# A decoder block on one core: state-space output with two matrices per group, a split gated product, constants loaded by SyncE, and new instruction orders

## The chip, the cores and the metric

The kernel runs on one core of one Trainium2 chip. The metric is the device time of one execution in microseconds (us). Before the change three runs gave 1078.19, 1079.68 and 1080.48, a median of 1079.68 us. A further execution was taken with the hardware profiler; all profile lines of the kernel before come from that one.

The names of the engines in the profile: PE is TensorE (matmuls), PEld its weight loads, DVE is VectorE, ACT is ScalarE, POOL is GpSimd, SP is SyncE, which here only issues DMAs.

## The reference

One layer of a decoder, float32, 512 tokens of width 1024:

```
h = h + 1/2 * SwiGLU_1(RMSNorm(h))                 # 1024 -> 2816 -> 1024
z = RMSNorm(h) @ W_in                              # q | k/v cmp, slc, win | gates | u (512 channels)
o = concat(NSA(8 heads x 64), S5(32 groups x 16 channels)) @ W_out
h = h + o
h = h + 1/2 * SwiGLU_2(RMSNorm(h))
h = h + sigmoid(RMSNorm(h) @ W_gate) * (p @ W_ple)
out = RMSNorm(h)
```

The S5 part, which the change is about, is for each of 32 groups a diagonal complex recurrence with 64 states, then a gelu and a gated linear unit:

```
state_t = a_bar * state_(t-1) + (B u_t) * b_coef   # complex, per group
y_t = Re(state_t) @ C_re^T - Im(state_t) @ C_im^T + d_skip * u_t
y = gelu(y);  out = y * sigmoid(y @ w_glu + b_glu) # w_glu is 512 x 512
```

## The kernel before, in words

**Layout.** Activations lie transposed: a tile of 128 features on the partitions by 512 tokens. The residual stream `h` is 8 such tiles. Weights come in `unit`s of 128 x 1024 fp32 (eight blocks of 128 x 128) from a packed tensor, loaded by SP into a ring of four buffers (`load_unit`, L111).

**Precision.** A product is done in a reduced fp32 type in three parts: `split` (L151, L152) makes `hi` by a cast on ACT and `lo` as the rest on DVE; the other operand is split the same way; `mm3` then does hi x hi, hi x lo, lo x hi. A product of two unsplit fp32 operands is the other way: the profile shows such a product as two records.

**Stages.** First FFN (to about 355 us), input projection with rotary products, key and value projections and the S5 input (to about 460), S5 interleaved with the score products (462 to 514), the gated linear unit (523 to 539), attention values and the output projection (from 544), second FFN (to 1011), the gate and the final norm. In the FFN most hidden tiles use a seven-product scheme, `prepare`, in which POOL issues DMAs that load weights and add a weight tile onto another (`raw<-raw`, L360).

**S5.** Time is cut in 64 chunks of 8 steps. The constants are computed on the chip in the first FFN, written to DRAM, and loaded again chunk by chunk: `s5i` holds per group a 128 x 128 input matrix `fd`, and cosines and sines `cd`, `sd` of 64 columns; `s5o` holds three 128 x 128 matrices `md`, `gd`, `gs` per group, where `gs` is `gd` with its two 64-partition halves exchanged (written by extra DMAs). `s5_in(j)` takes four groups at a time, eight times over: two loads by POOL (`si` of 512 KB, `so` of 768 KB, L886 and L888), a product with u (PE, `ps_C<-u,si`), a rotation by cos and sin on DVE (L894 to L897), the recurrence by four scans (L900) into `vv`, and one operation that multiplies `vv` by cos and by sin into the two halves of `z` (L904). `s5_out` adds per group three fp32 products, u with md, z cos with gd, z sin with gs. So the exchange of real and imaginary halves is done by the matrix `gs`. `vv` and the rotation's tiles have one buffer each, `si` three, `z` two.

**Gated unit.** `glu` takes four gelu tiles `yt` of 128 x 512, two raw weight units and 16 plain fp32 products of 512 columns (`ps_A<-yt,raw`); then tanh on ACT, and the gated tiles are split into `oh`, `ol` (L1092, L1094) for the output projection.

**What sets the order.** The program is traced first, and then `impose` chains each engine's instructions in the order that a table of numbers, `ENGINE_ORDER`, gives (L1627); a second table, `TILE_ORDER`, orders some users of shared buffers. So every engine, the two DMA issuers SP and POOL too, runs through a fixed list, and an instruction that waits holds back all that stand behind it on its engine. `rsqrt_steps` (L315 to L322) is the chain of a norm: `ones,acc` sums squares on PE, `ms` on DVE, `ri` on POOL, `nt`, `ri`, `dg` on DVE, and `dg,ones` on PE spreads the result.

Of the kernel before, what the change touches and what calls it, by code (L numbers as in the profile page):

```python
# [76 lines left out]
def block_kernel(ctx: ExitStack, tc: tile.TileContext, a: dict, out: bass.AP):  # L77
# [420 lines left out]
    s5i = dram.tile([128, NG, 256], F32, tag="s5i", name="s5i")  # L498
    fd, cd, sd = (s5i[:, :, i:j] for i, j in ((0, 128), (128, 192), (192, 256)))
    s5o = dram.tile([128, NG, 384], F32, tag="s5o", name="s5o")  # L500
    md, gd, gs = (s5o[:, :, i:j] for i, j in ((0, 128), (128, 256), (256, 384)))
    r8 = pers.tile([128, NG], F32, name="r8")

    def s5_constants(sp):
        if True:
# [175 lines left out]
            def make_m(c):  # L681
# [3 lines left out]
                for r in (0, 64):  # L685
                    nc.sync.dma_start(gs[64 - r:128 - r, chunk(c)], ko[r:r + 64])
# [30 lines left out]
            for c in range(2):  # L717
                gs_ = slice(16 * c, 16 * c + 16)
                tcs = sp.tile([128, 2, 16, 64], F32, tag="big0", name="tcs")
# [23 lines left out]
                nc.sync.dma_start(cd[:, gs_], tcs[:, 0])  # L743
                V.tensor_scalar(tcs[:, 1], tcs[:, 1], pos, None, OP.mult)
                nc.sync.dma_start(sd[:, gs_], tcs[:, 1])
# [48 lines left out]
    def mixer(ctx):  # L794
# [76 lines left out]
        for i in range(2):  # L871
            raw = tp.tile([128, SEQ], F32, tag=f"r{i + 1}", name="rope")
            nc.gpsimd.dma_start(raw, a["rope"][:, i])
            ropes.append(raw)
# [5 lines left out]
        zs = [s5w.tile([128, 2, GC, 64], F32, name="z", bufs=1, tag=f"z{i}") for i in range(2)]  # L880
        for z in zs:
            G.memset(z[:, :, :, 0:1], 0.0)

        def s5_in(j):
            si_ = s5w.tile([128, GC, 256], F32, tag="si", name="si", bufs=3)
            G.dma_start(si_, s5i[:, GC * j:GC * j + GC])  # L886
            so = s5w.tile([128, GC, 384], F32, tag="so", name="so")
            G.dma_start(so, s5o[:, GC * j:GC * j + GC])  # L888
            co, si = si_[:, :, 128:192], si_[:, :, 192:256]
            w = bank(TW, (128, GC, 64))  # L890
            for g in range(GC):
                mm(w[:, g], si_[:, g, 0:128], u8[:, GC * j + g], True, True)
# [10 lines left out]
            cs_ = si_.rearrange("p g (a c) -> p a g c", c=64)[:, 2:4, :, 0:63]  # L903
            V.tensor_tensor(z[:, :, :, 1:64], vv[:, None, :, 0:63].to_broadcast([128, 2, GC, 63]), cs_, OP.mult)  # L904
            return so, z

        def s5_out(j, yc, so, z):

            y = bank(TY, (128, GC // 2, 128))
            for i in range(GC // 2):  # L910
                for n, lhs in enumerate((u8[:, GC * j:GC * j + GC], z[:, 0], z[:, 1])):
                    for p in range(2):
                        g = 2 * i + p
                        mm(y[64 * p:64 * p + 64, i], lhs[:, g], so[:, g, 128 * n:128 * n + 128], n == 0, n == 2)
# [162 lines left out]
        def glu():  # L1077
            for m in range(4):
                yt = yts[m]
                gelu2(yt, yt, SEQ, ("r1", "r2")[m % 2])  # L1080
            yield
            for m in range(4):
                if m % 2 == 0:
                    raw = unit(True)
                o = bank("A")
                for k in range(4):
                    q = (m * 4 + k) % 8
                    mm(o, raw[:, q * 128:(q + 1) * 128], yts[k], k == 0, k == 3)
# [301 lines left out]
    with tc.tile_pool(name="gate", bufs=2, reuse_waits="tile") as gp:  # L1390
# [400 lines left out]
```

## Time and profile before

| what | value |
|---|---|
| median of three runs | 1079.68 us (1078.19 to 1080.48) |
| the profiled execution's own time | 1081.65 us |
| its span | 1079.9 us |
| busy: PE, DVE, ACT, POOL | 1042.9 (97%), 808.2 (75%), 521.9 (48%), 94.8 (9%) |
| granted TensorE clock, mean | 0.986 |
| moved by DMA | 151.13 MB, mean 140 GB/s |

A busy time is the sum over an engine's instructions; an average over the span mixes stages with different limits, which is why the prediction reads windows. In a timeline row stand start, duration, engine, line, operation, the names of what is written and read, shape, count, and in brackets the idle time before it with what ended it. In a row of groups stand busy us and mean ns, then the idle time before the group's instructions. PEclk is the clock that the chip granted to TensorE, as a share of full speed.

### The profile page before, as it was taken

What the parts mean: (1) busy time and instruction counts of PE and PEld (TensorE: products, weight loads), DVE (VectorE), ACT (ScalarE), POOL (GpSimd) and SP (SyncE); (2) the same over time, 40 slices, a digit from 0 to 9 for tenths busy, and PEclk for the clock granted to TensorE, in tenths of its full rate; (3) what the DMA queues carried; (4) which work ended last, traced back from release to release, by engine and by line L of the source; (5) the groups of instructions that cost most, each with busy time, mean ns of one, the idle gap of its engine ahead of it and who ended that gap; (6) DMA issues with size and microseconds to landing.
All of it is one profiled execution on the core that took longest, in us unless ns stands there. A gap on an engine that the chain in (4) does not pass through costs nothing.

```text
span 1079.9 us, 16852 instructions
## 1 busy us (share of the span) xinstructions
PE 1042.9 (97%) x6446; PEld 902.7 (84%) x6446; DVE 808.2 (75%) x1339; ACT 521.9 (48%) x911; POOL 94.8 (9%) x118
## 2 busy tenths in 40 slices
PE   6999999999999999999999999999999999999895
PEld 4788899799898888777577677998999899898795
DVE  7999876977887685699678968775576476476675
ACT  5334265335435532356789736463355245255431
POOL 5000010010001110011000001101011010100000
PEclk9999999999999999999899999999999999999898
DMA  9333356975747647867200066356356356445202
GB/s 313 108 94 110 82 152 158 252 183 136 205 109 187 222 133 206 210 212 251 66 32 20 15 210 175 93 142 179 84 143 178 91 117 160 114 122 172 59 30 69
DMA packets 86624, 151.13 MB, mean 140 GB/s; under 512 B 27648, under 2 KB 47104, under 8 KB 86544
## 3 DMA queue, kind: packets, MB, share of 16 engines
q1 hardware_dynamic: 72544, 120.23, 36.0%
q0 software_dynamic: 13152, 29.66, 13.5%
q8 instruction: 50, 0.82, 0.3%
q10 hardware_dynamic: 848, 0.17, 0.1%
q14 instruction: 30, 0.25, 0.1%
HBM read 123.27 MB, written 17.83 MB: 131 GB/s over the span
## 4 chain that ended last, share of the span: by engine, by line
PE 46%; issue 3%; DVE 2%; ACT 2%; POOLq 0%; POOL 0%; DVEq 0%; DMA 0%; SPq 0%; ACTq 0%
PE ps_C L130 13%; PE ps_A L130 13%; PE ps_B L130 12%; PE ps_D L130 8%; ACT hi L151 1%; DVE lo L152 0%; ACT pu L375 0%; DVE ple L1430 0%; DVE h L1107 0%; DVE h L478 0%; DVE acc L184 0%; ACT sq L183 0%; ACT eh L1242 0%; ACT e L1238 0%; DVE dg L322 0%
## 5 line engine op out<-in xcount | busy, mean ns | idle before, releaser
L151 ACT CAST hi<-raw 128x1024 fp32r<-128x1024 f32 (+2 forms) x201 | 208.7, 1042 | 260.2 <-PE ps_C L130 116.6
L152 DVE TENSOR_TENSOR lo<-raw,hi 128x1024 fp32r<-128x1024 f32 (+2 forms) x201 | 245.4, 1228 | 78.7 <-ACT hi L151 76.2
L130 PE MATMUL ps_C<-hq,hi 128*128 128x512 f32 x704 | 219.4, 393 | 0.7 <-DVE hq L345 0.2
L130 PEld LDWEIGHTS ps_C<-hq,hi 128*128 128x128 f32 x704 | 130.0, 189 | 28.2 <-DVE h L478 1.6
L130 PE MATMUL ps_A<-xh,hi 128*128 128x256 f32 (+1 forms) x456 | 143.1, 314 | 7.7 <-ACT xh L173 7.7
L130 PE MATMUL ps_A<-xl,hi 128*128 128x256 f32 (+1 forms) x456 | 142.2, 312 | 2.7 <-DVE xl L174 2.7
L130 PE MATMUL ps_A<-xh,lo 128*128 128x256 f32 (+1 forms) x456 | 142.3, 312 | 0.9 <-DVE lo L152 0.9
L130 PE MATMUL ps_C<-hq,lo 128*128 128x512 f32 x352 | 137.5, 391 | 0.0
L130 PEld LDWEIGHTS ps_A<-xh,hi 128*128 128x128 f32 x456 | 87.4, 192 | 12.9 <-ACT xh L173 7.7
L130 PEld LDWEIGHTS ps_A<-xl,hi 128*128 128x128 f32 x456 | 87.4, 192 | 9.3 <-DVE xl L174 4.0
L130 PEld LDWEIGHTS ps_A<-xh,lo 128*128 128x128 f32 x456 | 87.4, 192 | 6.0 <-DVE lo L152 1.4
L130 PE MATMUL ps_B<-sh,hi 128*128 128x256 f32 x280 | 81.1, 290 | 2.4 <-ACT pu L375 1.0
L130 PE MATMUL ps_B<-sh,lo 128*128 128x256 f32 x280 | 78.7, 281 | 0.2 <-DVE lo L152 0.2
L130 PE MATMUL ps_B<-sl,hi 128*128 128x256 f32 x280 | 78.6, 281 | 0.0
L130 PEld LDWEIGHTS ps_C<-hq,lo 128*128 128x128 f32 x352 | 66.4, 189 | 14.0
L478 DVE SCALAR_TENSOR_TENSOR h<-ps_C,h 128x512 f32<-128x512 f32 x64 | 44.2, 691 | 41.6 <-PE ps_C L130 40.3
L354 POOL DMA_DIRECT2D raw<-in_wpack x35 | 31.9, 910 | 408.1 <-DVE acc L184 131.6
L130 PE MATMUL ps_D<-sh,hi 128*128 128x256 f32 x220 | 62.1, 282 | 0.2 <-ACT p L375 0.2
L130 PE MATMUL ps_D<-sh,lo 128*128 128x256 f32 x220 | 62.1, 282 | 0.0
L130 PE MATMUL ps_D<-sl,hi 128*128 128x256 f32 x220 | 61.8, 281 | 0.0
L130 PEld LDWEIGHTS ps_B<-sh,hi 128*128 128x128 f32 x280 | 52.7, 188 | 6.7 <-ACT pu L375 5.4
L130 PE MATMUL ps_B<-xh,hi 128*128 128x512 f32 (+1 forms) x164 | 58.0, 353 | 0.1
(402 smaller groups left out, 2320.9 us busy)
## 6 DMA issues: line engine op xcount, KB each, us to landing
raw<-in_wpack SPq DMA_DIRECT2D x172, 512.0 KB, 4.3
raw<-in_wpack POOLq DMA_DIRECT2D x35, 256.0 KB, 4.7
raw<-raw POOLq DMA_DIRECT2D x35, 256.0 KB, 3.3
so<-s5o POOLq DMA_DIRECT2D x8, 768.0 KB, 6.7
si<-s5i POOLq DMA_DIRECT2D x8, 512.0 KB, 7.7
h<-in_xT SPq DMA_DIRECT2D x8, 256.0 KB, 5.5
s5i<-fs SPq DMA_DIRECT2D x4, 512.0 KB, 5.8
s5o<-gt SPq DMA_DIRECT2D x4, 512.0 KB, 4.7
```

Of the source, the lines that this page charges most:

```text
L130: return PE.matmul(o, lhsT, rhs, start=start, stop=stop, **kw)
L151: S.copy(hi[:, c], raw[:, c])
L152: V.tensor_tensor(lo[:, c], raw[:, c], hi[:, c].bitcast(F32), OP.subtract)
L354: nc.gpsimd.dma_start(a0[:, 1], src[:, 0:512], accum_op=OP.add)
L478: V.scalar_tensor_tensor(h[:, m, :], o, 0.5, h[:, m, :], OP.mult, OP.add)
```

## The change

1. **S5 output.** `z` becomes one rotated state: z = vv cos + x, where x is vv sin with its two 64-partition halves exchanged. DVE does it in four operations (L904 to L907) with a new tile `zt` in one buffer. `s5o` has two matrices, `gs` and its DMAs are gone, and `s5_out` does two products per group.
2. **Constants.** `s5i` becomes two tensors, the input matrices `s5f` and the cosines and sines `s5t`; the latter is written by two DMAs of 1 MB instead of four of 512 KB. The loads in `s5_in` (`fi`, `ti`, `so`, three buffers each, 256, 256 and 512 KB) and the two rotary tables are issued by SP instead of POOL.
3. **Gated unit.** The two weight units and the four gelu tiles are split into hi and lo, and the 16 products go by `mm3`: 48 matmuls.
4. **Orders.** Both tables are new for all five engines.

```diff
@@ constants
-    s5i = dram.tile([128, NG, 256], F32, tag="s5i", name="s5i")
-    fd, cd, sd = (s5i[:, :, i:j] for i, j in ((0, 128), (128, 192), (192, 256)))
-    s5o = dram.tile([128, NG, 384], F32, tag="s5o", name="s5o")
-    md, gd, gs = (s5o[:, :, i:j] for i, j in ((0, 128), (128, 256), (256, 384)))
+    fd = dram.tile([128, NG, 128], F32, tag="s5f", name="s5f")
+    td = dram.tile([128, NG, 2, 64], F32, tag="s5t", name="s5t")
+    s5o = dram.tile([128, NG, 256], F32, tag="s5o", name="s5o")
+    md, gd = (s5o[:, :, i:j] for i, j in ((0, 128), (128, 256)))
...
-                for r in (0, 64):
-                    nc.sync.dma_start(gs[64 - r:128 - r, chunk(c)], ko[r:r + 64])
...
-                nc.sync.dma_start(cd[:, gs_], tcs[:, 0])
                 V.tensor_scalar(tcs[:, 1], tcs[:, 1], pos, None, OP.mult)
-                nc.sync.dma_start(sd[:, gs_], tcs[:, 1])
+                nc.sync.dma_start(td[:, gs_], tct)
@@ mixer
-            nc.gpsimd.dma_start(raw, a["rope"][:, i])
+            nc.sync.dma_start(raw, a["rope"][:, i])
...
-        zs = [s5w.tile([128, 2, GC, 64], F32, name="z", bufs=1, tag=f"z{i}") for i in range(2)]
+        zs = [s5w.tile([128, GC, 64], F32, name="z", bufs=1, tag=f"z{i}") for i in range(2)]
...
         def s5_in(j):
-            si_ = s5w.tile([128, GC, 256], F32, tag="si", name="si", bufs=3)
-            G.dma_start(si_, s5i[:, GC * j:GC * j + GC])
-            so = s5w.tile([128, GC, 384], F32, tag="so", name="so")
-            G.dma_start(so, s5o[:, GC * j:GC * j + GC])
-            co, si = si_[:, :, 128:192], si_[:, :, 192:256]
+            fi = s5w.tile([128, GC, 128], F32, tag="fi", name="fi", bufs=3)
+            nc.sync.dma_start(fi, fd[:, GC * j:GC * j + GC])
+            ti = s5w.tile([128, GC, 2, 64], F32, tag="ti", name="ti", bufs=3)
+            nc.sync.dma_start(ti, td[:, GC * j:GC * j + GC])
+            so = s5w.tile([128, GC, 256], F32, tag="so", name="so", bufs=3)
+            nc.sync.dma_start(so, s5o[:, GC * j:GC * j + GC])
+            co, si = ti[:, :, 0], ti[:, :, 1]
...
             z = zs[j % 2]
-            cs_ = si_.rearrange("p g (a c) -> p a g c", c=64)[:, 2:4, :, 0:63]
-            V.tensor_tensor(z[:, :, :, 1:64], vv[:, None, :, 0:63].to_broadcast([128, 2, GC, 63]), cs_, OP.mult)
+            zt = s5w.tile([128, GC, 64], F32, tag="zt", name="zt", bufs=1)
+            V.tensor_tensor(z[:, :, 1:64], vv[:, :, 0:63], co[:, :, 0:63], OP.mult)
+            V.tensor_tensor(zt[64:128], vv[0:64], si[0:64], OP.mult)
+            V.tensor_tensor(zt[0:64], vv[64:128], si[64:128], OP.mult)
+            V.tensor_tensor(z[:, :, 1:64], z[:, :, 1:64], zt[:, :, 0:63], OP.add)
             return so, z
...
-                for n, lhs in enumerate((u8[:, GC * j:GC * j + GC], z[:, 0], z[:, 1])):
+                for n, lhs in enumerate((u8[:, GC * j:GC * j + GC], z)):
                     for p in range(2):
                         g = 2 * i + p
-                        mm(y[64 * p:64 * p + 64, i], lhs[:, g], so[:, g, 128 * n:128 * n + 128], n == 0, n == 2)
+                        mm(y[64 * p:64 * p + 64, i], lhs[:, g], so[:, g, 128 * n:128 * n + 128], n == 0, n == 1)
@@ glu
                 gelu2(yt, yt, SEQ, ("r1", "r2")[m % 2])
+                S.copy(oh[:, m], yt)
+                V.tensor_tensor(ol[:, m], yt, oh[:, m].bitcast(F32), OP.subtract)
             yield
             for m in range(4):
                 if m % 2 == 0:
-                    raw = unit(True)
+                    wu = unit()
                 o = bank("A")
                 for k in range(4):
                     q = (m * 4 + k) % 8
-                    mm(o, raw[:, q * 128:(q + 1) * 128], yts[k], k == 0, k == 3)
+                    sl = slice(q * 128, (q + 1) * 128)
+                    mm3(o, wu[0][:, sl], wu[1][:, sl], oh[:, k], ol[:, k], k == 0, k == 3)
@@ orders
 ENGINE_ORDER = {
     "PE": (
-        "65:42 31:3 -34:3 3:4 -7:3 28:12 -27 26:30 23:6 -29:3 26:42 26:45 15:3 -18:3 15:18 3:3 -6:3 3:21 65:18 "
...
```

Each number of such a row is a step through the traced program, with a count behind a colon; what they do is seen from the orders themselves. Three places matter to the prediction.

**DVE after the last rotary product.** `r` are the rotated halves, `ps_C,ti` is the S5 input product with its cosines or sines, `ra`, `rb` belong to the key and value projections, `QA` to the scores. Before:

```order
L959 TENSOR_TENSOR r_4266<-ps_B,cosr 128x512
L961 TENSOR_TENSOR r_4265<-r_4265,r_4266 128x512
L152 TENSOR_TENSOR lo<-raw,hi 128x840
L982 TENSOR_TENSOR ra<-ps_A,cosr 128x512
L983 TENSOR_TENSOR rb_4344<-ps_A,sinr 64x512
```

With the change:

```order
L964 TENSOR_TENSOR r_4256<-r_4256,r_4257 128x512
L894 TENSOR_TENSOR t_4278<-ps_C,ti 128x256
L963 TENSOR_TENSOR r_4254<-r_4254,rb_4255 128x512
L152 TENSOR_TENSOR lo<-raw,hi 128x840
L895 TENSOR_TENSOR t_4279<-ps_C,ti 64x256
L896 TENSOR_TENSOR t_4279<-ps_C,ti 64x256
L897 TENSOR_TENSOR t_4278<-t_4278,t_4279 128x256
L900 SCALAR_TENSOR_TENSOR vv<-r_103,t_4278 128x64 x4
L894 TENSOR_TENSOR t_4366<-ps_C,ti 128x256
L904 TENSOR_TENSOR z<-vv,ti 128x4x63
L905 TENSOR_TENSOR zt<-vv,ti 64x256
L906 TENSOR_TENSOR zt<-vv,ti 64x256
```

S5's first rows moved ahead of the key and value projections; on PE its first products with u likewise stand directly behind the last rotary projection. Further down, ahead of the first attention value product (`ps_D<-eh,VLc`), PE's old list has 15 matmuls on `ps_A<-oh` and `ol` (five triples); the new list has 72, of which 48 are the gated product.

**The loads of constants.** `raw<-raw` is the accumulation of the first FFN's last hidden tile, `so`, `si`, `rope` are loads. On POOL, as a piece of the difference (- before, + with the change):

```order
 L360 DMA raw<-raw 128x512 x2
-L888 DMA so<-s5o 128x1536
-L873 DMA rope<-in_rope 128x512
-L888 DMA so<-s5o 128x1536
-L873 DMA rope<-in_rope 128x512
-L886 DMA si<-s5i 128x1024
-L882 MEMSET z 128x8 x2
-L886 DMA si<-s5i 128x1024 x2
```

On SP with the change (`s5t` is the write of the cosines and sines, `raw<-in_wpack` a weight unit):

```order
L743 DMA s5t<-tcs 128x2048
L111 DMA raw<-in_wpack 128x1024 x11
L884 DMA fi<-s5f 128x512
L886 DMA ti<-s5t 128x512
L888 DMA so<-s5o 128x1024
L884 DMA fi<-s5f 128x512
L886 DMA ti<-s5t 128x512
L871 DMA rope<-in_rope 128x512 x2
L888 DMA so<-s5o 128x1024
```

The loads left POOL's list, where they stood right behind the accumulation, and stand on SP among its weight loads.

**The start of the gate.** `hq` are the second FFN's hidden tiles, `xh`, `xl` the input of the gate. PE before:

```order
L130 MATMUL ps_C<-hq,hi 128x512 x2
L130 MATMUL ps_C<-hq,lo 128x512
L130 MATMUL ps_D<-ones,acc 128x1 x4
L130 MATMUL ps_A<-xh,hi 128x256
L130 MATMUL ps_A<-xl,hi 128x256
L130 MATMUL ps_A<-xh,lo 128x256
```

With the change, where 15 gate products on `ps_A` stand between the last `hq` row and these:

```order
L130 MATMUL ps_A<-xh,lo 128x256
L130 MATMUL ps_B<-xh,hi 128x256
L130 MATMUL ps_B<-xl,hi 128x256
L130 MATMUL ps_B<-xh,lo 128x256
L130 MATMUL ps_D<-ones,acc 128x1 x4
L130 MATMUL ps_B<-xh,hi 128x256
```

So 18 gate products come ahead of `ones,acc` where there were none, and 51 between it and `dg,ones` where there were 24. On DVE the last sum of squares was followed at once by `ms`; now one `lo` stands ahead of that sum and three `lo` and an `xl` between it and `ms`.

More of the change, by code (lines that the diff above doesn't have):

```diff
@@ L718, in s5_constants @@
                 gs_ = slice(16 * c, 16 * c + 16)
-                tcs = sp.tile([128, 2, 16, 64], F32, tag="big0", name="tcs")
+                tct = sp.tile([128, 16, 2, 64], F32, tag="big0", name="tcs")
+                tcs = tct.rearrange("p g a c -> p a g c")
                 w1 = sp.tile([128, 2, 16, 32], F32, tag="bx", name="w1")
@@ L872, in mixer @@
             raw = tp.tile([128, SEQ], F32, tag=f"r{i + 1}", name="rope")
-            nc.gpsimd.dma_start(raw, a["rope"][:, i])
+            nc.sync.dma_start(raw, a["rope"][:, i])
             ropes.append(raw)
         u8 = s5w.tile([128, NG, 64], F32, tag="u8", name="u8", bufs=1)
-        zs = [s5w.tile([128, 2, GC, 64], F32, name="z", bufs=1, tag=f"z{i}") for i in range(2)]
+        zs = [s5w.tile([128, GC, 64], F32, name="z", bufs=1, tag=f"z{i}") for i in range(2)]
         for z in zs:
-            G.memset(z[:, :, :, 0:1], 0.0)
+            G.memset(z[:, :, 0:1], 0.0)
         def s5_in(j):
-            si_ = s5w.tile([128, GC, 256], F32, tag="si", name="si", bufs=3)
-            G.dma_start(si_, s5i[:, GC * j:GC * j + GC])
-            so = s5w.tile([128, GC, 384], F32, tag="so", name="so")
-            G.dma_start(so, s5o[:, GC * j:GC * j + GC])
-            co, si = si_[:, :, 128:192], si_[:, :, 192:256]
+            fi = s5w.tile([128, GC, 128], F32, tag="fi", name="fi", bufs=3)
[5 more added lines that the diff above has]
+            co, si = ti[:, :, 0], ti[:, :, 1]
             w = bank(TW, (128, GC, 64))
             for g in range(GC):
-                mm(w[:, g], si_[:, g, 0:128], u8[:, GC * j + g], True, True)
+                mm(w[:, g], fi[:, g], u8[:, GC * j + g], True, True)
             t1, t2 = (s5w.tile([128, GC, 64], F32, tag=n, name=n, bufs=1) for n in ("t1", "t2"))
```

307 rows, old and new, of tables (ENGINE_ORDER, TILE_ORDER) are left out of this document.

## The prediction

> **What bounds the kernel now.** I read the profile's page first, its busy shares and its chain of work that ended last:
>
> ```profile
> span 1079.9 us, 16852 instructions
> PE 1042.9 (97%) x6446; PEld 902.7 (84%) x6446; DVE 808.2 (75%) x1339; ACT 521.9 (48%) x911; POOL 94.8 (9%) x118
> PE 46%; issue 3%; DVE 2%; ACT 2%; POOLq 0%; POOL 0%; DVEq 0%; DMA 0%; SPq 0%; ACTq 0%
> ```
>
> TensorE (PE) is busy for 97% of the span and it alone makes up most of the chain, so as a whole the kernel is bound by matmuls. The 75% of VectorE (DVE) is a mean over stages, so next I read the busy times by stage. The columns after the window are its length, then PE, PEld, DVE, ACT and POOL busy, the granted clock (PEclk), DMA share and GB/s:
>
> ```profile
> 439.40:462.70 23.30, 22.97 (x129) 18.58 (x128) 17.91 (x28) 11.23 (x24) 0.00 (x0) 1.00 0.74 200
> 462.70:509.40 46.70, 46.25 (x406) 35.15 (x405) 44.79 (x111) 26.21 (x72) 5.94 (x11) 1.00 0.73 248
> 509.40:544.10 34.70, 31.93 (x167) 20.63 (x166) 24.99 (x59) 24.70 (x53) 0.00 (x0) 0.85 0.30 96
> 348.90:351.20 2.30, 0.06 (x1) 0.03 (x1) 1.17 (x3) 1.56 (x2) 0.00 (x0) 1.00 1.01 377
> 351.20:354.00 2.80, 2.80 (x17) 2.70 (x18) 1.59 (x2) 0.68 (x2) 0.00 (x0) 0.73 0.96 363
> 1011.40:1013.80 2.40, 0.17 (x1) 0.00 (x0) 1.39 (x2) 1.41 (x2) 0.00 (x0) 1.00 0.03 2
> 1013.80:1019.70 5.90, 5.15 (x26) 4.86 (x27) 3.74 (x11) 2.67 (x4) 1.95 (x1) 0.58 0.29 89
> ```
>
> The first three windows run from the end of the last rotary projection to the first split of attention weights. In the middle one, the state space (S5) stage, DVE is busy 44.79 of 46.70 us (96%) beside a PE busy 46.25: there are two bounds, and work taken from the one and laid on the other is not free. The last four windows are two places where PE stands still for over 2 us and then runs at a lower clock. The change touches all of them.
>
> **Part 1: matmuls removed.** The timeline of PE shows the gated product (raw fp32), one triple of the split product that replaces it (from an output product of the same shape), and S5's output for two pairs of groups:
>
> ```profile
> 523.23 15.62 PE L130 MATMUL ps_A<-yt,raw 128*128 128x512 f32 x32
> 541.40 0.40 PE L130 MATMUL ps_A<-oh,hi 128*128 128x512 f32 x1
> 542.10 0.40 PE L130 MATMUL ps_C<-QA,KAc 128*128 128x512 f32 x1
> 476.48 0.44 PE L130 MATMUL ps_D<-so,u 128*64 128x128 f32 x4
> 476.74 0.61 PE L130 MATMUL ps_D<-so,z 128*64 128x128 f32 x8
> 477.18 0.39 PE L130 MATMUL ps_D<-so,u 128*64 128x128 f32 x4
> ```
>
> Sixteen products took 15.62 us. A triple takes 542.10 - 541.40 = 0.70, so sixteen triples take 11.2: -4.4 us. Of S5's output, 12 records take 477.18 - 476.48 = 0.70; four go, 0.23, sixteen times over: -3.7. The row of 15.62 holds some slow clock that may come again, so I count -7.5 for both.
>
> **Part 2: what DVE gets instead.** Groups of DVE by shape between the two ends (us busy, mean ns), and two groups of the whole page:
>
> ```profile
> L904 DVE TENSOR_TENSOR z<-vv,si 128x504 f32<-128x504 f32 x8 | 5.5, 684 | 0.3
> L895 DVE TENSOR_TENSOR t<-ps_C,si 64x256 f32<-64x256 f32 x8 | 3.3, 418 | 0.2
> L897 DVE TENSOR_TENSOR t<-t,t 128x256 f32<-128x256 f32 x8 | 3.4, 422 | 0.2
> L1094 DVE SCALAR_TENSOR_TENSOR ol<-sg,oh 128x512 fp32r<-128x512 f32 x4 | 2.7, 685 | 0.1
> L151 ACT CAST hi<-raw 128x1024 fp32r<-128x1024 f32 (+2 forms) x201 | 208.7, 1042 | 260.2 <-PE ps_C L130 116.6
> L152 DVE TENSOR_TENSOR lo<-raw,hi 128x1024 fp32r<-128x1024 f32 (+2 forms) x201 | 245.4, 1228 | 78.7 <-ACT hi L151 76.2
> ```
>
> Per chunk of four groups, one operation of 684 ns becomes four: two on 128 partitions at 422, two on 64 at 418, 1.68 us in all, so +1.0 a chunk, +8.0 over eight. Splitting two weight units adds 2 x 1.23 = 2.5, and four splits of the gelu output 4 x 0.685 = 2.7. That is +13.2 nominal; neighbours overlap a little at their ends, as the start times show, so +12.5. ACT gets two casts of 1.04 and four half as wide, some 4.5 us; it was busy 24.70 of 34.70 in its fullest window here and bears them, save where DVE waits for one of them in turn.
>
> Whether PE's gain arrives is decided by DVE between these two ends (timeline of DVE):
>
> ```profile
> 438.70 0.69 DVE L958 TENSOR_TENSOR rb<-ps_B,sinr 128x512 f32<-128x512 f32 x1 [3.02 <-PE ps_B L130]
> 544.12 0.69 DVE L1244 TENSOR_TENSOR el<-e,eh 128x512 fp32r<-128x512 f32 x1 [0.53 <-ACT eh L1242]
> ```
>
> From 439.4, where the first ends, to 544.1 are 104.7 us, with 17.91 + 44.79 + 24.99 = 87.7 busy and 17.0 idle (5.4, 1.9 and 9.7 in the three windows). With +12.5 it is 100.2. Adding up the rows that the new order puts between the same two operations, each at its group's mean, I get 102.2: 74.6 from the first S5 product to the last z, 27.6 after it. So at most 2.5 us of the old length are left as slack. The new order does one thing against it: S5 starts straight after the last rotary product, ahead of the key and value projections, and these fill DVE's gaps. At the idle share of the S5 window (1.9 in 46.7, 4%) 74.6 us hold 3.0 of idle. For the 27.6 after it the bounds are nothing and the 9.7 of the old tail; I take 3.5, nearer to the low end, because the gated product's triples stand among score products and no longer as one block of 15.6 us for which the rest has to wait. That makes 102.2 + 6.5 = 108.7, **+4.0 us** (bounds: idle 2 gives -0.5, the old 17 gives +14.5). So the 7.5 us of PE work buy nothing there by themselves: they become PE waits for DVE. Part of the room is used, though. Ahead of the first attention value product the old order has 5 triples of the output projection, the new one 24 triples on the same tile of which 16 are the gated product: three more, which PE needn't do later, 3 x 0.70 = **-2.0**.
>
> **Part 3: loads from SyncE (SP).** At the end of the first FFN, POOL's rows, ACT's and PE's:
>
> ```profile
> 343.15 0.86 POOL L360 DMA_DIRECT2D raw<-raw  x1 [9.72 <-DVE lo L152]
> 343.81 0.76 POOL L888 DMA_DIRECT2D so<-s5o  x1
> 349.38 0.62 ACT L362 CAST ah<-raw 128x512 fp32r<-128x512 f32 x1 [2.63 <-DMA raw<-raw]
> 351.20 0.36 PE L130 MATMUL ps_B<-xh,ah 128*128 128x256 f32 x1 [2.24 <-DVE t L418]
> raw<-raw POOLq DMA_DIRECT2D x35, 256.0 KB, 3.3
> so<-s5o POOLq DMA_DIRECT2D x8, 768.0 KB, 6.7
> raw<-in_wpack SPq DMA_DIRECT2D x172, 512.0 KB, 4.3
> ```
>
> The accumulating transfer issued at 343.15 landed some 6.2 us later where 3.3 is usual. A load of 768 KB was issued 0.66 behind it, and the DMA engines were full (share 1.01 in 348.9 to 351.2). ACT, DVE and PE then waited in line. PE lost 2.24 us, and at a granted 0.73 in the next window 0.27 x 2.80 = 0.76 more: 3.0. In the new order POOL has no load there. SP issues the first 512 KB `so` only after eleven weight loads and two pairs of fi and ti that follow the last write of constants. That write is now one of 1 MB and may still meet the accumulation. Bounds 0 and -3.0; I take **-2.5**, since the one culprit whose issue lies next to the late transfer is gone. Behind these loads on SP stand weight loads: a load that waits for its buffer (three each of fi, ti, so) holds back the weights behind it, and PE would wait for hi and lo. A unit of weights feeds eight triples, 8 x 0.70 = 5.6 us of PE, and the ring holds four, so up to 22 us of work cover a late load: I cost it at nothing. With the cover gone it is one landing, 4.3 us, at one place.
>
> The granted clock fell here after a gap of 2.24 us. The Trainium skill ("TensorE: Matmul & The Clock Gate", Why this matters for your kernels) asks only for no gaps over about 3 us; by it the stall would be worth 2.24 and not 3.0. The row of 0.73 says otherwise, and the measurement decides.
>
> **Part 4: start of the gate.** The timeline of PE and DVE at the end of the second FFN:
>
> ```profile
> 1013.80 1.08 PE L130 MATMUL ps_D<-ones,acc 128*128 128x1 f32 x8 [2.23 <-DVE acc L184]
> 1016.27 0.58 PE L130 MATMUL ps_A<-xh,lo 128*128 128x256 f32 x1 [0.75 <-DVE lo L152]
> 1021.13 1.21 PE L130 MATMUL ps_D<-dg,ones 128*128 128x512 f32 x2
> 1022.30 0.28 PE L130 MATMUL ps_B<-xl,hi 128*128 128x256 f32 x1
> 1023.35 0.28 PE L130 MATMUL ps_B<-xl,hi 128*128 128x256 f32 x1
> 1013.06 0.69 DVE L184 TENSOR_TENSOR acc<-acc,sq 128x512 f32<-128x512 f32 x1 [0.76 <-ACT sq L183]
> 1015.00 1.22 DVE L152 TENSOR_TENSOR lo<-raw,hi 128x1024 fp32r<-128x1024 f32 x1
> 1019.28 0.48 DVE L322 TENSOR_SCALAR dg<-ident,ri 128x128 f32<-128x128 f32 x2
> ```
>
> PE waits 2.23 us for the sum of squares, 0.75 for the low part of the gate's first weights, and runs 5.15 us of work at 0.58, which costs 0.42 x 5.15 = 2.2: 5.2 in all. Now 18 gate products stand between the last FFN product and `ones,acc`. At full speed nine take 1023.35 - 1022.30 = 1.05, so 18 fill 2.1 of the 2.23; their lo is formed before the sum of squares on DVE. 51 more follow before `dg,ones`, 6.0 us, so PE gets there at about 1013.8 + 0.5 + 6.0 = 1020.3. On DVE, however, three lo of 1.2 and an xl now stand between the sum of squares and `ms`, the first step to dg. If the sum ends 0.4 later than now, at 1014.2, `ms` comes at about 1018.3 instead of 1014.9, and dg, 4.8 after it now with two lo in between (one of them beside POOL's step), needs some 3.2: 1021.5. PE waits about 1.2 there. Bounds -2 (a lo or a weight load is late as well) and -5.2; with the 1.2 off the upper I take **-4.0**.
>
> **The rest.** One row of the waits of PE is the start's:
>
> ```profile
> PE ps_A L130 <- ACT xh L173: 7.7, 1, 7.7
> ```
>
> The start is ordered anew (five input loads ahead of the first weights). This wait is for the first data in any order: it may grow by what comes first now, while later waits for input shrink; I put it at 0 ± 2. The other stages are reshuffled under a PE that is full: 0 ± 3.
>
> Sum: +4.0 - 2.0 - 2.5 - 4.0 = -4.5. The profiled execution took 1081.65 us by its own time (1.75 around the span), so it would become 1077.2; it lies 1.97 above the median of 1079.68, so on the scale of the runs the forecast is **1075.2 us**.
>
> **The rivals.** (a) *DVE becomes the bound in the S5 stretch and PE pays.* For: 96% busy there already, and four operations in line per chunk where there was one, with vv, zt and t held in one buffer each. Against: the earlier start of S5. If the idle between the two ends stays at 17.0, they lie 119.2 apart, +14.5: 1079.7 + 14.5 - 8.5 = 1085.7. It decides from 11 us of idle on, where the sum is zero. (b) *DVE packs tightly and the stalls go entirely.* Idle 2 gives -0.5; with -2.0, -3.0 and -5.2 that is 1069.0. For: 4% idle in the old S5 window. Against: the 9.7 of the tail, chains between ACT and DVE that no reordering shortens. (c) *The stalls stay.* The same bytes still cross the same 16 engines, which were at 1.01: if the first stall stays and half of the second, 4.0 - 2.0 - 2.0 = 0, 1079.7. The Trainium skill ("DMA: Bandwidth & Descriptors", Issuing engines are not separate DMA queues) speaks for it: another issuing engine saves issue time alone. By it the -2.5 would be 0, unless the loads also move in time, as they do in the new order; the trace of before can't show that.
>
> **How the numbers follow.** Forecast 0.45 (its own range 1071 to 1079.5), (a) 0.23, (b) 0.17, (c) 0.15. Within 0.2%, 1077.5 to 1081.8, is what a measurement can't tell from no change. The forecast gives about 0.38 to faster and 0.07 to no change, (b) 0.17 and (c) 0.05 to faster, (c) 0.08 to no change, (a) almost all to slower and the remains of (c) there: 0.60, 0.15, 0.25. The range reaches to most of (a) and of (b): 1067 to 1085.
>
> **What would show it.** In the profile of the changed kernel: the ends `rb` of the last rotary and the first `el` 106 to 111 us apart (over 114: (a); under 105: (b)); DVE at 95% or more over S5's 75 us, PE with some 6 to 10 us of waits for z, zt or lo there, which were absent; no wait over 1 us for `raw<-raw` near 349, and none near 1011 to 1017, with the granted clock near 1.0 in both. I would be wrong most simply if PE in the S5 stretch waits for weights behind SP's loads, or if the idle in the tail isn't 3.5.

## The result and the profile after

Four runs of the changed kernel gave a median of 1063.68 us (1062.13 to 1064.68), four of the kernel before on the same chip 1080.04. The ratio is 0.9851 [0.9832, 0.9869]: 1.5% faster. The forecast was 1075.2 with a range of 1067 to 1085, so the direction was right, and the time lies outside the range, on the fast side. The profiled execution took 1064.68 us, 16.97 less than the one before; the forecast had 4.5.

The page of the changed kernel, its busy shares and its chain:

```profile
span 1062.9 us, 16719 instructions
PE 1026.4 (97%) x6398; PEld 899.3 (85%) x6398; DVE 814.2 (77%) x1369; ACT 524.7 (49%) x917; POOL 81.9 (8%) x100
PE 86%; DVE 8%; issue 2%; ACT 2%; DMA 1%; POOL 0%; SPq 0%; POOLq 0%; DVEq 0%; ACTq 0%
```

PE is busy for 97% of the span, as it was before, and yet the kernel is 17 us shorter. The busy share didn't see what was gained. So the time has to be taken apart by stage. These are the busy times by windows of the kernel before; each window ends where the same instruction stands in both kernels (first and last product on `hq` of the first FFN, last rotary, first attention split, last addition of the output projection, last product of the second FFN, end):

```profile
92.20:382.00 289.80, 285.63 (x1886) 258.88 (x1886) 229.67 (x318) 133.11 (x208) 31.16 (x43) 0.99 0.63 166
382.00:438.70 56.70, 56.70 (x254) 46.75 (x253) 35.58 (x54) 15.41 (x18) 2.28 (x4) 1.00 0.62 172
438.70:544.10 105.40, 101.85 (x701) 74.93 (x700) 88.38 (x197) 62.83 (x148) 5.94 (x11) 0.95 0.60 187
544.10:647.00 102.90, 102.44 (x487) 77.26 (x486) 84.58 (x157) 76.17 (x175) 0.90 (x1) 1.00 0.20 65
647.00:1011.18 364.18, 360.59 (x2365) 327.34 (x2364) 240.63 (x314) 170.30 (x267) 35.82 (x40) 1.00 0.50 131
1011.18:1079.80 68.62, 54.72 (x416) 52.30 (x414) 45.55 (x108) 22.25 (x42) 3.34 (x3) 0.87 0.20 62
```

And of the changed kernel:

```profile
98.40:381.60 283.20, 283.20 (x1899) 258.86 (x1898) 229.50 (x325) 132.22 (x209) 28.45 (x37) 1.00 0.62 167
381.60:436.30 54.70, 54.70 (x246) 44.86 (x244) 34.96 (x53) 15.27 (x18) 2.03 (x2) 1.00 0.55 159
436.30:545.00 108.70, 100.23 (x675) 77.22 (x675) 99.81 (x230) 68.99 (x161) 0.00 (x0) 0.94 0.57 160
545.00:642.00 97.00, 97.00 (x464) 74.69 (x463) 83.83 (x157) 73.33 (x167) 0.94 (x1) 1.00 0.25 79
642.00:998.40 356.40, 356.15 (x2365) 326.57 (x2364) 239.06 (x313) 171.14 (x268) 34.86 (x40) 1.00 0.50 133
998.40:1062.90 64.50, 51.44 (x416) 49.58 (x414) 44.66 (x108) 22.22 (x42) 2.43 (x3) 0.93 0.21 66
```

| stretch | before | after | difference | forecast |
|---|---|---|---|---|
| start, to the first product on `hq` | 92.2 | 98.4 | +6.2 | 0 ± 2 |
| first FFN, to its last product | 289.8 | 283.2 | -6.7 | -2.5 |
| norm and input projection, to the last rotary | 56.6 | 54.8 | -1.9 | 0 |
| S5, scores, gated unit, to the first `el` | 105.4 | 108.7 | +3.3 | +4.0 |
| attention values and output projection | 103.2 | 97.5 | -5.8 | -2.0 |
| second FFN | 363.8 | 356.0 | -7.9 | 0 |
| gate and final norm | 68.7 | 64.5 | -4.2 | -4.0 |
| sum | 1079.9 | 1062.9 | -17.0 | -4.5 |

(The table goes by the exact start of each instruction, the windows by rounded ones.) The most telling pair is the fifth row of windows: the second FFN has the same 2365 matmuls in both, 99% busy before and 100% after, and lasts 7.8 us less. The forecast had called such stages "reshuffled under a PE that is full".

**Where those 8 us were.** The timeline of PE in the kernel before, at one hidden tile of the second FFN:

```profile
728.62 0.28 PE L130 MATMUL ps_B<-xl,ah 128*128 128x256 f32 x1
728.73 0.28 PE L130 MATMUL ps_B<-xh,al 128*128 128x256 f32 x1
729.18 0.38 PE L130 MATMUL ps_B<-sh,hi 128*128 128x256 f32 x1 [0.17 <-ACT pu L375]
729.40 0.28 PE L130 MATMUL ps_B<-sl,hi 128*128 128x256 f32 x1
729.52 0.28 PE L130 MATMUL ps_B<-sh,lo 128*128 128x256 f32 x1
```

and ACT's copy for which it waits:

```profile
728.76 0.37 ACT L375 COPY pu<-ps_B 128x256 f32<-128x256 f32 x1
```

A matmul's record lasts 0.28 us, but the next one starts 0.12 behind it. So a record that is followed by nothing still counts as busy for 0.16 more. Between 728.73 and 729.18 stand 0.45 us instead of 0.12, and the next step is 0.22 instead of 0.12: 0.43 lost, of which the profile books 0.17 as idle. Where the late step is shorter than 0.16, nothing at all is booked. PE's groups by shape over this stage, the kernel before:

```profile
L130 PE MATMUL ps_B<-sh,hi 128*128 128x256 f32 x160 | 46.2, 288 | 1.4 <-ACT pu L375 0.3 <-ACT ps_B L391 0.2
```

and the change:

```profile
L130 PE MATMUL ps_B<-sh,hi 128*128 128x256 f32 x160 | 45.3, 283 | 0.0
```

The waits are gone. To add them up I took, for each kind of matmul (operands and shape), the usual (most frequent) distance from its start to the next matmul's start, over both kernels, and summed what stands above it. From the second FFN's first matmuls to its end the kernel before has 50 places with over 0.06 us, 9.45 us together; the change has 14, 1.8 us. Over the window of the first FFN the excess falls from 11.5, the stall at 349 among it, to 2.3; the stage gets only 6.7 shorter, since by the usual distances 2.5 us more matmul work stands in it now. In the second FFN of the kernel before about half of the excess stands at products that need the copies of L375, the rest at others, such as those that need a `lo` or an `hq`. The Trainium skill ("Perfetto Trace Analysis", Identifying the Most-Contended Engine) warns that the busy share of matmuls is not a good measure of how near a kernel is to its limit, because they are pipelined; this trace agrees, with 97% before and after.

### The profile page after: what moved, and what is told of

Its sections match the earlier page's. It is cut to its first block, busy times and chain, and to the rows that moved or that the text cites. A ratio compares the mean times of both kernels' runs of the same rounds, so it can differ in the third digit from the quotient of the medians.

```text
span 1062.9 us, 16719 instructions
## 1 busy us (share of the span) xinstructions
PE 1026.4 (97%) x6398; PEld 899.3 (85%) x6398; DVE 814.2 (77%) x1369; ACT 524.7 (49%) x917; POOL 81.9 (8%) x100
## 4 chain that ended last, share of the span: by engine, by line
PE 86%; DVE 8%; issue 2%; ACT 2%; DMA 1%; POOL 0%; SPq 0%; POOLq 0%; DVEq 0%; ACTq 0%
PE ps_C L130 27%; PE ps_B L130 23%; PE ps_A L130 22%; PE ps_D L130 14%; DVE nmax L1155 1%; DVE lo L152 1%; DVE vv L900 1%; ACT xh L173 0%; DMA ti<-s5t 0%; DMA raw<-in_wpack 0%; DMA u<-ud 0%; PE ps_C L676 0%; ACT xn L183 0%; DMA h<-in_xT 0%; ACT hi L151 0%
## 5 line engine op out<-in xcount | busy, mean ns | idle before, releaser
L130 PE MATMUL ps_A<-xh,hi 128*128 128x256 f32 (+1 forms) x456 | 142.6, 313 | 10.4 <-ACT hi L151 10.4
L130 PEld LDWEIGHTS ps_C<-hq,hi 128*128 128x128 f32 x704 | 127.1, 188 | 23.5 <-issue 0.8
L130 PEld LDWEIGHTS ps_A<-xh,hi 128*128 128x128 f32 x456 | 87.2, 191 | 16.0 <-ACT hi L151 10.4
L130 PE MATMUL ps_B<-xh,lo 128*128 128x512 f32 (+1 forms) x160 | 55.8, 349 | 0.0
```

Source lines behind the costliest of these rows:

```text
L130: return PE.matmul(o, lhsT, rhs, start=start, stop=stop, **kw)
```

## The experiments

Ratios are to the kernel before, run on the same chip; the change has 0.9851. "Order of" means that the instructions of a stretch were put, on all five engines, in the relative order that the other kernel gives them; nothing else differs (in experiments 1 and 2 one entry of `TILE_ORDER` changes with them).

**1 and 2. Is the second FFN's gain its order?** The new order alone in the kernel before, and the old order in the changed one:

```diff
 # kernel before, from the first to the last product of the second FFN, all engines
-order of the kernel before
+order of the change
```

> The kernel before, with only the instructions of the second FFN standing in the changed kernel's relative order on every engine; nothing else is changed. Theory 1, short waits: in the kernel before PE waits some 0.3 us at many hidden tiles for a copy out of PSUM by ACT or for a lo by DVE, and about 0.1 more until the next matmuls follow at their usual distance; the new order puts other products there. Summed over start-to-start distances this is 11.2 us from the norm to the last FFN product before and 4.1 after, so it expects 7 us less, 1073. Theory 2, the second FFN runs faster because of something else in the change (less traffic, other buffers, an earlier supply of weights): no change, 1080.

Measured 1069.84 us, ratio 0.9915 [0.9901, 0.993]: 9 us of the 17, from an edit that touches no instruction, only their order in a stage that the change's code doesn't touch.

```diff
 # changed kernel, the same stretch
-order of the change
+order of the kernel before
```

> The changed kernel, with the second FFN's instructions in the relative order of the kernel before on every engine. Theory 1, short waits: they come back, 7 us more, 1071. Theory 2: no change, 1063.7.

Measured 1072.3, ratio 0.9937 [0.9922, 0.9952]; the stage's end moved back from 998.40 to 1007.49. Both directions agree at 8 to 9 us, so the cause is shown: the order of this stage, with the short waits as what it removes. The stage itself hardly scatters: in the profiled executions of this document, those two kernels' own aside, it took 362.9 to 363.7 us in the five with the old order and 355.7 to 355.9 in the six with the new one. The first of the two also answers a question on the gate, where the old stall stayed. Its timeline of PE:

```profile
1002.55 1.05 PE L130 MATMUL ps_D<-ones,acc 128*128 128x1 f32 x8 [2.23 <-DVE acc L184]
```

and the window of 5.9 us behind it:

```profile
1002.60:1008.50 5.90, 4.86 (x28) 4.65 (x29) 3.82 (x11) 2.61 (x4) 1.95 (x1) 0.74 0.28 89
```

The same gap of 2.23 us is followed by a granted 0.74 where the prediction's row had 0.58. The stall at 349 us shows the same in this execution, where nothing was changed so far: PE's gap is 2.18 us there and the clock behind it stays at 1.00, where the prediction's rows had 2.24 and 0.73:

```profile
350.40:353.20 2.80, 2.80 (x20) 2.63 (x21) 1.94 (x3) 0.77 (x2) 0.00 (x0) 1.00 0.91 354
```

What a gap costs in clock is not a constant of its length.

**3. The first FFN's order alone, POOL's loads left behind the accumulation.**

```diff
 # kernel before, first FFN from 92 us on, all engines; the loads stay on POOL
-order of the kernel before
+order of the change
```

> The kernel before, with the instructions of the first FFN from about 92 us on in the changed kernel's relative order; the loads of constants stay on POOL right behind the accumulation. Theory 1, short waits: 11.3 us of excess distance become 1.6 with the change; of these 4.2 are the stall at 349 us, which stays here if the loads on POOL are its cause. It expects 5.5 us less, 1074.5, with the stall still there; 9.7 less, 1070, if the order alone removes the stall. Theory 2: no change, 1080.

Measured 1074.39, ratio 0.9953 [0.9938, 0.9968], some 5 us less. In the profile the last product of the first FFN came 7.7 us earlier; 1.6 were given back in the norm behind it, where PE waits for the sum of squares. And the stall at 349 was gone, and ACT's cast waits for nothing, though POOL's rows still stand together. POOL's timeline:

```profile
341.02 0.86 POOL L360 DMA_DIRECT2D raw<-raw  x1 [9.19 <-DVE lo L152]
341.56 0.88 POOL L888 DMA_DIRECT2D so<-s5o  x1
```

The cast of what the accumulation brings, on ACT:

```profile
345.21 0.62 ACT L362 CAST ah<-raw 128x512 fp32r<-128x512 f32 x1
```

So the `so` load behind the accumulation was not the culprit that the prediction had named. What had moved away is a DMA on SP, issued at 312.40 here. In the kernel before it is the second of these two, the write of the sines (L745), issued 0.4 us behind the accumulation at 343.15:

```profile
339.33 0.38 SPq L743 DMA_DIRECT2D s5i<-tcs  x1
343.54 0.38 SPq L745 DMA_DIRECT2D s5i<-tcs  x1
```

**4. The write alone, later.** In the kernel before, the last write of constants goes behind three weight loads:

```diff
 L743 DMA s5i<-tcs 128x16x64
+L111 DMA raw<-in_wpack 128x1024 x3
 L745 DMA s5i<-tcs 128x16x64
-L111 DMA raw<-in_wpack 128x1024 x11
+L111 DMA raw<-in_wpack 128x1024 x8
```

> The kernel before with one edit in SP's order: the last write of cosines and sines (issued at 343.54 us, 0.4 behind the accumulation that came late) stands three weight loads later; the load on POOL stays where it is. If that write, in pieces of 256 bytes, delays the accumulation: the wait of 2.2 us at 349 us goes, 3 us less, 1076. If the load on POOL does it, as the prediction had it: the wait stays, 1079.5. The three weight loads may be issued earlier and take the write's place as disturbers; then part of the wait stays.

Ten runs gave 1075.54, ratio 0.9977 [0.9967, 0.9988]: 2.6 us. POOL's timeline:

```profile
342.93 0.86 POOL L360 DMA_DIRECT2D raw<-raw  x1 [9.71 <-DVE lo L152]
343.60 0.75 POOL L888 DMA_DIRECT2D so<-s5o  x1
```

and ACT's:

```profile
346.44 0.62 ACT L362 CAST ah<-raw 128x512 fp32r<-128x512 f32 x1
```

The accumulation lands 3.3 us after its issue where it took 6.2, with the `so` load still 0.67 behind it. The culprit is that write, and the size of the stall, 2.5, was right (the interval is 1.3 to 3.6 us). The write goes out in pieces of 64 columns, 256 bytes; whether the small pieces matter, or only its 512 KB at that moment, was not tried.

**5. The loads on POOL again.** In the changed kernel:

```diff
-            nc.sync.dma_start(fi, fd[:, GC * j:GC * j + GC])
+            G.dma_start(fi, fd[:, GC * j:GC * j + GC])
 # the same for ti, so and the rotary tables; on POOL they stand behind the last accumulation
```

> The changed kernel with the loads of fi, ti, so and of the rotary tables issued by POOL again, the first eleven right behind the first FFN's last accumulation, as before; SP has them no more. The prediction's step (the loads on POOL delay the accumulation): the wait of 2.2 us at about 349 us is back, with a granted clock below 1 behind it, 2.5 to 3 us more, 1066.5. Rival: the order of the accumulations and of the products behind them decides, as it did when the first FFN's new order alone took the stall away with the loads still on POOL: no such wait, 1063.7.

Measured 1068.04, ratio 0.9904 [0.9888, 0.9921]: slower than the change by some 4 to 6 us, though its profiled execution, the fastest of four, was only 0.4 us behind. The stall at 349 did not come back. The loss is elsewhere, in the S5 stage: in that execution the stretch from the last rotary to the first `el` took 111.4 us instead of 108.7, while the start happened to be 1.6 shorter. POOL's timeline:

```profile
465.01 0.53 POOL L888 DMA_DIRECT2D so<-s5o  x1 [21.64 <-PE ps_D L130]
465.53 0.54 POOL L884 DMA_DIRECT2D fi<-s5f  x1
```

and PE's:

```profile
470.42 1.34 PE L130 MATMUL ps_C<-u,fi 128*128 128x64 f32 x8 [3.24 <-DMA fi<-s5f]
```

A load of `so` waits 21.64 us for its buffer and holds the next `fi` behind it; PE needs that one at 467 and gets it at 470.4. In the change SP issues the `fi` of 453.03 and 457.04 ahead of the `so` of 466.43. So by these rows the move to SP buys another place in a list, not another engine. The Trainium skill ("DMA: Bandwidth & Descriptors", Issuing engines are not separate DMA queues) has it that another issuer saves no more than issue time. The medians of the two pages agree on the transfer, 5.3 us from issue to landing for a `so` on POOL here and 5.5 on SP in the change; the rows above show that the place in the list counts.

**6. S5 with two matrices, alone, in the kernel before's order.**

```diff
-            V.tensor_tensor(z[:, :, :, 1:64], vv[:, None, :, 0:63].to_broadcast([128, 2, GC, 63]), cs_, OP.mult)
+            V.tensor_tensor(z[:, :, 1:64], vv[:, :, 0:63], co[:, :, 0:63], OP.mult)
+            V.tensor_tensor(zt[64:128], vv[0:64], si[0:64], OP.mult)
+            V.tensor_tensor(zt[0:64], vv[64:128], si[64:128], OP.mult)
+            V.tensor_tensor(z[:, :, 1:64], z[:, :, 1:64], zt[:, :, 0:63], OP.add)
```

> The kernel before with the two-matrix output alone: DVE's four operations stand in place of its one, PE has a third fewer S5 output products, the writes of the third matrix are gone, loads stay on POOL, all orders otherwise as before. Theory DVE: the S5 window of 46.7 us has 1.9 us of DVE idle, so 8 more us of DVE lengthen it by 4 to 6, and the 3.7 us that PE saves are only more waiting: 1084 to 1086. Rival PE: PE is busy 46.25 of these 46.7, and what it saves arrives: 1076.

Measured 1089.18, ratio 1.0097 [1.0081, 1.0113]. The stretch from the last rotary to the first `el` grew from 105.4 to 114.6 us; grown among PE's waits, from 0.3 and 0.2 us, are two for ACT's exponentials of the scores (L1153), which write where PE wants to go on:

```profile
PE ps_B L130 <- ACT ps_B L1153: 3.7, 5, 1.6
PE ps_C L130 <- ACT ps_C L1153: 3.5, 3, 1.9
```

ACT in turn waits up to 5 us for `nmax`, the reduction on DVE, among whose rows S5's four now stand (timeline of ACT):

```profile
476.93 0.66 ACT L1153 ACTIVATE ps_B<-ps_B,nmax 128x512 f32<-128x512 f32 x1 [4.96 <-DVE nmax L1150]
```

**7. The split gated product, alone.**

```diff
+                S.copy(oh[:, m], yt)
+                V.tensor_tensor(ol[:, m], yt, oh[:, m].bitcast(F32), OP.subtract)
...
-                    mm(o, raw[:, q * 128:(q + 1) * 128], yts[k], k == 0, k == 3)
+                    mm3(o, wu[0][:, sl], wu[1][:, sl], oh[:, k], ol[:, k], k == 0, k == 3)
```

> The kernel before with the split gated product alone: 48 matmuls where the 16 stood, the casts and differences of the four gelu tiles at 511 to 524 us, those of the two weight units from 514 and 520 us on, all else in the order of before. By the rows the block takes 11.2 instead of 15.6 us; it starts 1 to 2 us later, since the last gelu tile must be split first. If PE's saving arrives: 3 us less, 1076.5. If the added 5 us of DVE, ahead of the score products and the combination weights, decide instead: no change or up to 2 us more, 1079 to 1081.

Measured 1087.15, ratio 1.0083 [1.0068, 1.0098], a miss: it takes matmul time away and costs 8 us. The stretch lasts 113.4 us. The waits of PE that are new or grown most (the second was 0.8) are

```profile
PE ps_A L130 <- ACT sg L1094: 3.7, 1, 3.7
PE ps_D L922 <- ACT ysb L917: 2.0, 1, 2.0
```

for the tanh of the gated unit and for a copy of S5's output, both on ACT, which now has the added casts to do as well. In experiments 6 and 7 the granted clock over the stretch was 0.91, where it was 0.95 before, so part of the loss is slower matmuls. By themselves, each in the old order, the two changes of the mixer lengthen the stretch by 9.2 and 7.9 us; in the new order both together by 3.3. Neither change of the code had a price here apart from its order.

**8. How far does DVE set the pace in that stretch?** In the changed kernel the sine part of the state is left out (no `zt`, no addition), which takes three of DVE's four new operations away:

```diff
-            V.tensor_tensor(zt[64:128], vv[0:64], si[0:64], OP.mult)
-            V.tensor_tensor(zt[0:64], vv[64:128], si[64:128], OP.mult)
-            V.tensor_tensor(z[:, :, 1:64], z[:, :, 1:64], zt[:, :, 0:63], OP.add)
```

> The changed kernel without the three exchange operations of each chunk (both zt and the addition), so the state's sine part is left out; PE has all its products. It takes 24 operations, about 10 us, from DVE between the last rotary product and the first attention value product. If DVE sets the pace there: the two ends come 5 to 8 us closer than 108.7, 1056 to 1058.5. If PE does: no change, 1063.7.

Measured 1061.97, ratio 0.9844 [0.982, 0.9867], not apart from the change's. In the profile the stretch is 106.6 us instead of 108.7:

```profile
435.80:542.40 106.60, 100.98 (x674) 78.25 (x674) 91.03 (x205) 68.91 (x161) 0.00 (x0) 0.92 0.56 163
```

DVE has 91.03 us of work where the change has 99.81, some 9 us less, and the stretch is 2.1 shorter, not 5 to 8. Even the 2.1 may be scatter: with the change's own order the stretch took 108.5 and 108.9 us in the profiled executions of experiments 2 and 9, and 106.8 in that of experiment 10, with a granted clock of 0.94 in the former two and 0.97 in the latter. So DVE doesn't set the pace by itself. PE is as full as DVE there (100.23 of 108.70 in the change, in part at a lower clock), and the reading that it takes over as soon as DVE has room fits, but no run tried it.

**9. The gate's sums first.** In the changed kernel PE's four sums come ahead of the 18 gate products again:

```diff
 L130 MATMUL ps_C<-hq,lo 128x512
+L130 MATMUL ps_D<-ones,acc 128x1 x4
 L130 MATMUL ps_A<-xh,hi 128x256
...
 L130 MATMUL ps_B<-xh,lo 128x256
-L130 MATMUL ps_D<-ones,acc 128x1 x4
```

> The changed kernel with one edit in PE's order: the four products of the sum of squares stand ahead of the 18 gate products again. The prediction's step: PE waits 2.2 us for the sum again, the 18 come behind it, the clock falls after the gap: 2.1 us more with a clock that holds and up to 4 with one that doesn't, 1066 to 1067.7. Rival: dg comes late by DVE's three lo in any case, so that the 18 only move into a wait that PE has anyway: no change, 1063.7.

Measured 1066.84, ratio 0.989 [0.9875, 0.9905], 3 to 4 us slower than the change, and the wait is back in the timeline of PE:

```profile
1001.73 1.05 PE L130 MATMUL ps_D<-ones,acc 128*128 128x1 f32 x8 [2.52 <-DVE acc L184]
```

**10. The old start.** What runs ahead of the first product on `hq`, in the changed kernel:

```diff
 # changed kernel, all engines, to 98 us
-order of the change
+order of the kernel before
```

> The changed kernel, with what runs before the first FFN's first output product (98 us) in the relative order of the kernel before. The changed kernel comes to that product 6.2 us later than the kernel before and has 6.9 us more of waits of PE ahead of it. If that is a plain loss, it ends about 6.5 us earlier than the changed kernel: 1057. Rival: the late start is the price of the free first FFN behind it (small operations for the constants moved ahead), and the time comes back there as waits: 1063.7.

Measured 1057.18 (1056.55 to 1060.15), ratio 0.9806 [0.9787, 0.9825]: faster than both kernels, than the change by 5 to 6.5 us. PE's waits in the first 98.4 us of the change:

```profile
PE ps_A L130 <- ACT hi L151: 10.4, 1, 10.4
PE ps_A L130 <- DVE lo L152: 4.0, 1, 4.0
```

and in the first 92.2 us here:

```profile
PE ps_A L130 <- ACT xh L173: 8.3, 1, 8.3
PE ps_A L130 <- DVE xl L174: 2.6, 2, 1.7
```

With five input loads ahead of them the first weights land at 8.9 us instead of 5.0, and their `hi` comes late: that is the wait of 10.4. The wait of 4.0, which ends at 28.31, has another cause. The `hi` of those weights was done at 20.05, but the new order put small operations for the constants ahead of their `lo` on DVE, and seven of these took 1.15 to 1.34 us each where some 0.18 is usual, all while POOL was adding `acc` tiles, from 16.38 to 26.41. So the `lo` starts 7 us after its `hi`. The last of the seven and that `lo`, in the timeline of DVE in the change:

```profile
25.15 1.29 DVE L530 TENSOR_SCALAR ex<-ex 128x32 f32<-128x32 f32 x1
27.04 1.22 DVE L152 TENSOR_TENSOR lo<-raw,hi 128x1024 fp32r<-128x1024 f32 x1
```

Which of the two causes weighs more was not tried, since the experiment takes back both. The first product on `hq` is back at 92.20, and nothing later takes the gain away.

**11. One more step on it.** In that kernel the first gated triple, for which PE waits 3.4 us (`ol`), goes behind 14 products that follow it:

```diff
-L130 MATMUL ps_A<-oh,hi 128x512
-L130 MATMUL ps_A<-ol,hi 128x512
-L130 MATMUL ps_A<-oh,lo 128x512
 L130 MATMUL ps_C<-KA,QA 128x384
...
+L130 MATMUL ps_A<-oh,hi 128x512
+L130 MATMUL ps_A<-ol,hi 128x512
+L130 MATMUL ps_A<-oh,lo 128x512
```

> The changed kernel with the old start (1057.2) and one more edit: the first triple of the gated product, at which PE waits 3.4 us for ol, stands behind the 14 products that follow it. If PE's waits there lie on the path: up to 3 us less, 1054.5. If DVE sets the pace: PE only waits at another place, 1057.2.

Measured 1057.94, ratio 0.9816 [0.9795, 0.9837]: no gain. The wait only changed its name:

```profile
PE ps_C L130 <- ACT ps_C L1158: 4.3, 1, 4.3
```

The scores that now come first wait as long, for ACT's exponentials and, as far as the rows suggest, through them for DVE. The stretch is 108.9 us where it was 106.8, but 108.5 to 108.9 is what it took in the change's order too.

## Why the prediction was right and wrong

**Right in size, partly by luck: the stretch around S5.** Forecast +4.0, measured +3.3 (+1.4 in the profile of experiment 10, whose order there is the same). Two bounds, PE's saved matmul time not arriving, is what the runs show: experiments 6 and 7 cost time although they take matmuls away. The two numbers inside were off in opposite ways and nearly cancelled: DVE was busy 99.1 (99.81 less 0.69 of the rotary row itself) instead of 102.2, and idle 8.9 instead of 6.5. That DVE alone decides there is too strong; taking 9 us of its work away gave 2.1 at most. The S5 stage's window in the change:

```profile
442.00:512.00 70.00, 63.93 (x476) 48.32 (x477) 68.01 (x160) 43.09 (x105) 0.00 (x0) 0.97 0.73 219
```

and PE's waits there between 436.3 and 545:

```profile
PE ps_A L130 <- DVE ol L1085: 3.7, 2, 3.4
PE ps_A L130 <- ACT sg L1097: 1.6, 1, 1.6
PE ps_D L130 <- DVE z L907: 0.6, 1, 0.6
```

DVE is at 97%, over the 95 I had named, and PE stands for 6.1 us of the 70, in the 6 to 10 that I expected; but the long wait is for the gelu's `ol` and hardly any for `z`. Rival (a) needed 11 us of idle; there were 8.9. Rival (b) named the nearest time, 1069.0, but DVE did not pack as tightly as it had it, with 2 us of idle.

**Right: the gate.** Forecast -4.0, measured -4.2, and experiment 9 gives 3 to 4 back (2.7 of it in this stage of its profile). In detail one step failed: I had the `lo` of the 18 products ready in time, but PE waits 1.68 for one of them ahead of the sums, against the sign of no wait over 1 us; for `dg`, where I had put 1.2, it doesn't wait. The clock stays at 1.00 where it was 0.58. Two rows of PE's waits and sums, one of `dg`, and the window:

```profile
1000.72 0.38 PE L130 MATMUL ps_A<-xh,lo 128*128 128x256 f32 x1 [1.68 <-DVE lo L152]
1002.71 0.95 PE L130 MATMUL ps_D<-ones,acc 128*128 128x1 f32 x8
1009.55 1.02 PE L130 MATMUL ps_D<-dg,ones 128*128 128x512 f32 x2
998.40:1012.00 13.60, 11.92 (x95) 11.18 (x94) 9.28 (x18) 7.62 (x9) 1.04 (x1) 1.00 0.49 156
```

**Right in size, wrong in cause: the stall at 349.** It is gone, and it was worth 2.6 (experiment 4). The step "the one culprit whose issue lies next to the late transfer" failed: I took POOL's load for the culprit and kept the write of constants on SP only as something that "may still meet the accumulation", although the old one was issued 0.4 us after the accumulation, closer than the load. Because that write moved as well (in the change the last one is issued at 317.58, over 28 us ahead of the last accumulation), the forecast came out right by luck. Rival (c) missed, since the stall did go, but its argument held: with the loads back on POOL the stall stays away (experiment 5), so their move gave nothing here.

**Wrong: "the other stages are reshuffled under a PE that is full: 0 ± 3".** This is the step that threw the time out of the range. The second FFN gave -7.9, the first FFN -4.2 beyond its stall, the input stages -1.9: 14 us from orders whose effect I set to nothing because the busy share was 97% and the list of waits short. Experiments 1 to 3 show the two FFNs' part to be the order alone. The 1.9 was not tried; by the usual distances 1.7 of it is matmul work that now stands elsewhere, and the first FFN has 2.5 more. The numbers that could have told it were in the trace of before: 11.5 us of excess distance in the first FFN and 9.45 in the second.

**Mis-sized: the output projection, -2.0.** It gave -5.8. By the usual distances some 3.5 us of matmul work had moved ahead of the first `el`, where I counted three triples, 2.0: score products (`KA,QA` and `QA,KA`) moved as well. A further 2.3 came from short waits, as in the FFNs. No run tried this stage alone, so the split is a count and not shown by an experiment.

**Wrong: the start, 0 ± 2.** It cost 6.2. "This wait is for the first data in any order" was the error: the order of the loads decides whether inputs or weights come last, the order on DVE when a `lo` is made, and experiment 10 gets the 6.2 back. The start took back a quarter of the 23.1 us that the rest gained; without it the forecast would have been off by more.

## What to carry to other kernels

A busy share near 100% on PE doesn't mean that it is full: compare the distance from one matmul's start to the next with the usual distance for that kind, stage by stage, and what stands above it is the room that an order can win. Price a reordering by splicing one stage's order into the other kernel, in both directions; price a change of the code only together with an order made for it. When a transfer is late, list what every queue issued around it, not only the queue that it is on, and when a wait is removed, look for its new name before counting the gain.

## What the runs showed of the hardware

- A short wait of PE costs more than itself: behind the one at 729.18 the next matmul started 0.22 us later instead of 0.12, and the first one's record lasts 0.38 instead of 0.28.
- With a write of 512 KB in pieces of 256 bytes issued 0.4 us behind it, an accumulating transfer of 256 KB took 6.2 us to land, against 3.3 with the write moved away; a load of 768 KB issued 0.67 behind it on its own queue did not delay it.
- After the same gap of 2.23 us the granted clock over the next 5.9 us was 0.58 in one kernel and 0.74 in another, and over 2.8 us behind gaps of 2.24 and 2.18 at the same place it was 0.73 and 1.00, so the loss behind a gap isn't set by its length alone. Why they differ was not tried.
- Small DVE operations on 128x32, usually some 0.18 us, took 1.15 to 1.34 each in seven cases while POOL was adding 128x512 tiles; three more in the same time took 0.18. Why was not tried.
